# Logsumexp over heads: two of 64 tiles loaded through GpSimd in parts of 120 and 8 rows, each batch stored in one DMA

## Chip, cores, metric

One core of a Trainium2 chip. The metric is the device time of one execution, in microseconds.

## The reference

```python
def reference(x, bias):            # x [8, 2048, 2048] f32, bias [8, 256] f32
    x_heads = x.reshape(B, S, H, Dh).transpose(0, 2, 1, 3) + bias[None, :, None, :]
    x_tiled = np.repeat(x_heads, 2, axis=2)
    mx = x_tiled.max(axis=-1, keepdims=True)
    return mx.squeeze(-1) + np.log(np.exp(x_tiled - mx).sum(axis=-1))   # [8, 8, 4096]
```

Per row and head it is the logarithm of the sum of 256 exponentials, and each result is written twice. 134 MB are read from HBM, the chip's main memory, and 1 MB is written, so the loads of x are most of the traffic.

## The kernel before

x is cut into 64 tiles of 256 rows. A tile is `[128 partitions, 2 rows, 2048]` f32, 2 MB, so each partition receives 16 KB that lie together in HBM. The tile lies in SBUF, the on-chip memory of 128 partitions. There are 9 tile buffers. Loads and stores are issued by SyncE (SP).

```python
NBUF = 9
STORE_ROWS = [                      # one list per batch: rows of each store, 64 in all
    [15, 14, 13, 12, 10],
    [11, 9, 16, 16, 12],
    [16, 16, 16, 8, 8],
    ...
]
def load(t):
    for k0, k1, c0, c1 in pieces(t):            # one piece, but for the last two tiles
        nc.sync.dma_start(out=xts[t % NBUF][:, k0:k1, c0:c1], in_=rows_of(t)[:, k0:k1, c0:c1])
...
for t in range(NBUF):
    load(t)
...
def finish(b, src, n_blk, k_rows, base, i, engine):     # once per batch of 8 tiles
    ...                             # transpose on TensorE, logarithm on ScalarE into rs
        step, parts = n, STORE_ROWS[b]
    for rows in parts:              # one DMA each, rows of 2 KB
        ...
        engine.dma_start(out=ov, in_=iv)
...
for t in range(T):
    # TensorE adds the bias to the first two heads of the tile; ScalarE takes exp of
    # everything and sums those two heads; VectorE weighs and sums the other six heads
    ...
            for k in range(k0, k1):
                for c in range(w0, c1, Dh):
                    weigh(xt[:, k, c : c + Dh], c // Dh, sum_at(k, c // Dh))
    if t + NBUF < T:
        load(t + NBUF)
```

The softmax here doesn't subtract the row's maximum and nothing guards it: scores larger than these inputs give would overflow.

## Time and profile before

| | before |
|---|---|
| median of 2 runs | 342.58 us (342.24 to 342.92) |
| span in the profile | 341.4 us |
| load of one tile, undisturbed | 4.89 us, 428 GB/s |
| ScalarE's work on one tile | 4.44 us |
| last load of tile 61 lands | 321.5 us; then 19.9 us of computation |

From the page of the kernel before: the span; the busy share of the 16 DMA engines (in tenths) and the GB/s they moved, in 40 equal slices; the chain of work that ended last, by line; and ScalarE's exponential (busy us, mean ns of one, idle before it and what ended that). In all views PE is TensorE, ACT ScalarE, DVE VectorE, POOL GpSimd, and SPq the queue of SyncE.

```profile
span 341.4 us, 3425 instructions
...
DMA  8999999999999999999999999999999999999910
GB/s 302 430 430 429 427 430 427 426 425 426 424 429 429 430 429 419 431 426 429 430 424 425 428 428 427 379 402 428 430 419 389 397 428 429 396 380 397 366 57 16
...
DMA xt<-in_x_dram 39%; PE ps L160 2%; ACT xt L174 2%; ACT ps L166 1%; ACT res L209 0%; DVE junk L180 0%; SPq L100 0%; PE ps L155 0%; PE tps L196 0%; DVE Rz L180 0%; ACTq L174 0%; DVEq L318 0%
...
L174 ACT ACTIVATE xt<-xt 128x3072 f32<-128x3072 f32 (+3 forms) x70 | 177.7, 2541 | 24.5 <-DMA xt<-in_x_dram 19.9
```

The engines are busy until the last two slices and move about 428 GB/s, but for some dips late in the run. The exponential waited for little but loads.

One more record matters. The page counts 16 DMA engines, and in the trace each load of 128 rows has 16 completion events. They are read here as one of each engine, so that a lagging engine shows up as one event behind the others (in the table by 1.11 us at tile 8 and by 7.81 us at tile 61):

```
completion of a tile's load, us behind the median of its 16 engines, kernel before
tile   median    the four slowest engines
   8    47.33    0.27  0.39  0.75  1.11
  18    96.27    0.39  0.76  1.74  3.08
  42   214.73    0.93  1.29  2.29  8.18
  61   313.68    1.68  2.17  2.22  7.81
```

### The profile page before, as it was taken

Reading aid. Unit: us, or ns where it says so; the run is one execution under the profiler, and the core shown is the slowest. Engines: PE = TensorE matmul, PEld = TensorE weight load, DVE = VectorE, ACT = ScalarE, POOL = GpSimd, SP = SyncE. Lnnn points to the kernel's source line nnn. Section 1 sums busy time; section 2 is a strip of 40 time slices with the busy share of each in tenths; the row PEclk is TensorE's granted clock in tenths of the full one; section 3 lists DMA queues with packets and bytes.
Section 4 is the critical chain, followed back from the end, with each engine's and each line's share of the span. In section 5 each row is a group of like instructions: output and inputs, shape, how many; then the busy total and the mean of one; then the engine's idle time right before and its main releaser. Section 6 shows DMA issues by size and latency. Waiting matters only on the chain. (4 is left out here: it accounts for less than half of the span.)

```text
span 341.4 us, 3425 instructions
## 1 busy us (share of the span) xinstructions
PE 235.2 (69%) x410; PEld 69.7 (20%) x410; DVE 271.6 (80%) x1538; ACT 295.2 (86%) x597; POOL 10.4 (3%) x22
## 2 busy tenths in 40 slices
PE   6295788767786767775767775965775665775791
PEld 2121122112121112221121221321221221221220
DVE  0429999898887888887889688787798698797795
ACT  2389999998997998987997997998998998998895
POOL 6000000000000000000000000000000000000004
PEclk9999856885868885888885886588888888888585
DMA  8999999999999999999999999999999999999910
GB/s 302 430 430 429 427 430 427 426 425 426 424 429 429 430 429 419 431 426 429 430 424 425 428 428 427 379 402 428 430 419 389 397 428 429 396 380 397 366 57 16
DMA packets 11545, 135.50 MB, mean 397 GB/s; under 512 B 1913, under 2 KB 2185, under 8 KB 3329
## 3 DMA queue, kind: packets, MB, share of 16 engines
q1 hardware_dynamic: 11168, 135.17, 94.8%
q0 software_dynamic: 352, 0.10, 0.1%
q14 instruction: 20, 0.16, 0.1%
q8 instruction: 3, 0.05, 0.1%
q10 hardware_dynamic: 2, 0.01, 0.0%
HBM read 134.23 MB, written 1.05 MB: 396 GB/s over the span
## 5 line engine op out<-in xcount | busy, mean ns | idle before, releaser
L180 DVE CUSTOM_DVE_ANT_0 junk<-xt,w_rep 128x256 f32<-128x256 f32 x768 | 270.8, 422 | 65.7 <-ACT xt L174 65.6
L160 PE MATMUL ps<-xt,ident 128*128 128x512 f32 x256 | 184.3, 859 | 88.6 <-DMA xt<-in_x_dram 88.3
L174 ACT ACTIVATE xt<-xt 128x3072 f32<-128x3072 f32 (+3 forms) x70 | 177.7, 2541 | 24.5 <-DMA xt<-in_x_dram 19.9
L166 ACT ACTIVATE ps<-ps 128x256 f32<-128x256 f32 x256 | 94.6, 369 | 11.7 <-PE ps L160 6.7
L160 PEld LDWEIGHTS ps<-xt,ident 128*128 128x128 f32 x256 | 57.4, 248 | 173.2 <-DMA xt<-in_x_dram 124.2
L180 DVE DVE_READ_ACCUMULATOR2_ANT R<- 128x1 f32 x744 | 61.9, 83 | 0.0
L155 PE MATMUL ps<-b,ones 3*128 3x512 bf16 x128 | 46.6, 447 | 6.2 <-DVE R L180 6.2
L166 ACT ACTIVATION_READ_ACCUMULATOR ps<-ps 128x1 f32 x256 | 48.6, 190 | 0.0
L155 PEld LDWEIGHTS <-ones 3*128 3x128 bf16 x128 | 7.5, 97 | 74.5 <-issue 66.7
L230 POOL DMA_DIRECT2D out_dram<-res x8 | 4.0, 505 | 324.1 <-ACT res L209 324.1
L136 PE MATMUL ps<-brow,ones 1*128 1x512 f32 x6 | 5.5, 1074 | 3.2 <-DMA brow<-in_bias_dram 3.2
L209 ACT ACTIVATE res<-tps 64x512 f32<-64x512 f32 (+3 forms) x11 | 5.9, 540 | 1.4 <-PE tps L196 0.9
L143 ACT ACTIVATE w_rep<-ps 128x512 f32<-128x512 f32 x3 | 1.8, 597 | 5.5 <-PE ps L136 5.5
L196 PEld LDWEIGHTS tps<-ident,R 128*64 128x64 f32 (+1 forms) x16 | 2.7, 166 | 8.9 <-issue 4.7
L196 PE MATMUL tps<-ident,R 128*64 128x128 f32 (+1 forms) x16 | 4.3, 363 | 0.0
L196 PE MATMUL tps<-ident,Rz 128*8 128x128 f32 x2 | 0.7, 374 | 4.7 <-DVE Rz L180 4.7
L136 PEld LDWEIGHTS ps<-brow,ones 1*128 1x128 f32 x6 | 1.8, 321 | 5.3 <-issue 5.3
L110 ACT ACT_TABLE_LOAD x1 | 1.3, 1283 | 0.7 <-PEq L307 0.7
L132 POOL DMA_DIRECT2D b<-bparts x3 | 1.6, 553 | 0.0
L196 PEld LDWEIGHTS tps<-ident,Rz 128*8 128x8 f32 x2 | 0.2, 82 | 5.2 <-DVE Rz L180 2.6
L129 POOL TENSOR_TENSOR brest<-brest,bparts 1x512 f32<-1x512 f32 x1 | 1.1, 1146 | 0.1
L127 POOL TENSOR_TENSOR brest<-brow,bparts 1x512 f32<-1x512 f32 x1 | 1.1, 1144 | 0.1
(15 smaller groups left out, 5.7 us busy)
## 6 DMA issues: line engine op xcount, KB each, us to landing
xt<-in_x_dram SPq DMA_DIRECT2D x62, 2048.0 KB
xt<-in_x_dram SPq DMA_DIRECT2D x2, 1024.0 KB
xt<-in_x_dram SPq DMA_DIRECT2D x2, 512.0 KB
xt<-in_x_dram SPq DMA_DIRECT2D x3, 256.0 KB
out_dram<-res SPq DMA_DIRECT2D x17, 32.0 KB
xt<-in_x_dram SPq DMA_DIRECT2D x2, 128.0 KB
out_dram<-res POOLq DMA_DIRECT2D x8, 12.0 KB, 1.7
out_dram<-res SPq DMA_DIRECT2D x3, 24.0 KB
```

Source lines behind the costliest of these rows:

```text
L110: nc.scalar.add_instruction(mybir.InstLoadActFuncSet(name=nc.get_next_instruction_name(), act_func_set_id=set_idx,))
L132: nc.gpsimd.dma_start(out=b3[i : i + 1, :], in_=bparts[:, i])
L136: nc.tensor.matmul(ps[i], lhsT=ones, rhs=brow[:, CPE + c : CPE + c + MM], start=True, stop=True,)
L143: nc.scalar.activation(out=w_rep[:, c : c + MM], in_=ps[i], func=ACT.Exp)
L155: nc.tensor.matmul(p[:, 0:CPE], lhsT=ones3, rhs=b3, start=True, stop=False)
L160: nc.tensor.matmul(p[:, 0:CPE], lhsT=ident, rhs=v, start=False, stop=True)
L166: nc.scalar.activation(out=p[:, c : c + Dh], in_=p[:, c : c + Dh], func=ACT.Exp, accum_out=dst(h),)
L174: nc.scalar.activation(out=v, in_=v, func=ACT.Exp)
L180: nc.vector.tensor_tensor_reduce(out=j, in0=v, in1=w_rep[:, c : c + Dh], scale=1.0, scalar=0.0, op0=ALU.mult, op1=ALU.add, accum_out=dst,)
L196: nc.tensor.transpose(out=tps[i][0:nr, k], in_=src(k), identity=ident)
L209: nc.scalar.activation(out=rv, in_=tv, func=ACT.Ln)
L230: engine.dma_start(out=ov, in_=iv)
```

## The change

The intent can be read from the code. Its constant `SLOW = 3` names one DMA engine as the slow one. GpSimd is to load two tiles so that this engine gets no part of them: 120 rows to the other 15 engines, and the last 8 rows, too, to others. The code counts in `turn`, modulo 16, where it supposes GpSimd's next row to go, and short "filler" DMAs are to turn that count to the right place. Four fillers on SP are added, and each batch is stored in one DMA of 64 rows.

```diff
+SPECIAL = (16, 40)
+SLOW = 3
...
+    fill = [sb.tile([16, 160], F32, name=f"fill{i}") for i in range(8)]
...
+    def turn_by(engine, rows):
+        i = turn[1]
+        turn[1] += 1
+        n = 128 + i
+        engine.dma_start(out=fill[i][0:rows, 0:n], in_=x[0, 0:rows, 0:n])
+
+    def turn_to(at):
+        if (at - turn[0]) % 16:
+            turn_by(nc.gpsimd, (at - turn[0]) % 16)
+        turn[0] = at
+
+    def load_special(t):
+        dst, src = xts[t % NBUF], rows_of(t)
+        cut = P - P // 16
+        turn_to(SLOW + 1)
+        nc.gpsimd.dma_start(out=dst[0:cut], in_=src[0:cut])
+        turn[0] = SLOW
+        turn_to(SLOW + 1)
+        nc.gpsimd.dma_start(out=dst[cut:P], in_=src[cut:P])
+        turn[0] = SLOW + 1 + P - cut
+        if t == SPECIAL[0]:
+            for rows in (1, 2, 3, 4):
+                turn_by(nc.sync, rows)
+
     def load(t):
+        if t in SPECIAL:
+            load_special(t)
+            return
...
-            step, parts = n, STORE_ROWS[b]
+            step, parts = n, [nr]
```

More of the change, by code (lines that the diff above doesn't have):

```diff
@@ L22 @@
 LAST_CUTS = [[0, 1024, 2048], [0, 512, 1024, 1536, 1792, 2048]]
-STORE_ROWS = [
-    [15, 14, 13, 12, 10],
-    [11, 9, 16, 16, 12],
-    [16, 16, 16, 8, 8],
-    [16, 16, 16, 9, 7],
-    [16, 16, 16, 10, 6],
-    [16, 16, 16, 11, 5],
-    [16, 16, 16, 12, 4],
-]
+SPECIAL = (16, 40)
+SLOW = 3
 @with_exitstack
@@ L96, in rows_of @@
         return v.rearrange("(k p) d -> p k d", k=K)
+    turn = [0, 0]
+    def turn_by(engine, rows):
[19 more added lines that the diff above has]
+                turn_by(nc.sync, rows)
     def load(t):
+        if t in SPECIAL:
+            load_special(t)
+            return
         for k0, k1, c0, c1 in pieces(t):
```

## The prediction

> **What bounds the kernel now.** The DMA engines, and among them one straggler. The slice view shows them nine tenths busy until the last stores; the chain of waits is mostly "DMA xt<-in_x_dram". In the instruction records ScalarE needs 4.44 us per tile unheld, but its period is 4.89 us, idling on the load before most tiles from 14 on: compute has slack, the loads have not.
>
> The completion events of the loads (16 per load, one per engine) show the straggler. A tile takes 4.89 us on every engine, yet one engine lands last in every tile: 1.1 us after the median at 33 us, 3.1 at 77 us, 5.2 at 141 us, 8.2 at 214 us. The lag grows in steps of about 1.0 us each 25 us. The instruction-fetch packets (queue 14, 8 KB) recur at the same beat (54, 76, 101, 127, 154 us), which fits VectorE's 1538 instructions. [...]Tile 61 lands at 321.5 us, at 313.7 in the median and 315.9 on the next slowest engine. From 321.5 on ScalarE waits on no load for the last 20 us. So the straggler sets the time.
>
> Which engine is it? It completes also in the stores of 5 and 4 rows[...].
>
> **What the change does.** [...]Each skip spares the straggler 8 packets of 611 ns, 4.9 us. Single stores take its rows per batch from 5 to 4, about 0.7 us in all, and free issue slots: only 8 SP loads and stores may be in flight, and bursts of 5 stores now cost the fast engines 0.3 to 1.2 us of stall at each batch from 215 us on. That is off the critical path while the straggler leads.
>
> **A doubt.** In the built program the one-row fillers of 129 and 135 elements are split as 3x43 and 15x9[...]. No trace here decides.
>
> **Sum**, for the landing of tile 61, with a tail of 20 us unchanged:
> - one skip: 321.5 - 4.9 - 0.7 = 315.9; time about 337 us (likeliest)
> - two skips: straggler 311, but the second slowest engine, freed of stalls, 313.5 to 314; about 335
> - none: about 342.5
>
> Tiles 16 and 40 arrive early and delay their neighbours by up to 4.9 us; ScalarE wins that back at 0.45 us per tile.
>
> **Predicted: 337.0 us, 334.3 to 343.3.** Chances: faster by over 2% 0.22, within 2% 0.74, slower 0.04.
>
> **What would show it.** Right: the straggler's lag drops by 4.9 us at tile 16 (perhaps at 40), tile 61 lands near 316, the tail stays 20 us, fast engines' stalls at batch ends vanish. Wrong: the lag grows through both tiles as before (another engine skipped), or GpSimd's tile packets take more than 611 ns, or ScalarE is still behind after tile 55.

The sum comes to 321.5 - 4.9 - 0.7 = 315.9 us for the landing of tile 61, hence, with the tail of 20 us and the 1.2 us by which the time of the kernel before exceeds its span, to about 337 us. Its numbers stand, as estimates: 4.9 us are 8 packets of 611 ns, the 128 packets of a tile over 16 engines; 0.7 us is about one store row less for the straggler in each of 8 batches, at the 84 ns that a packet of 2 KB took in the median in the kernel before. The 4 rows per batch are 64 rows over the 16 completions that such a store has in the kernel after; the 5 were seen in the kernel before, as the straggler completes in every store of a batch. It is the last even in the store of 5 rows (8.16 us behind the median) and in that of 4 (1.00 us).

## More of the kernel before

The windows of the kernel before around the place of the first changed tile (last two columns: busy share of the DMA engines, GB/s):

```profile
...
core 0: us, PE busy (x) PEld busy (x) DVE busy (x) ACT busy (x) POOL busy (x), PEclk, DMA share, GB/s
40.00:58.00 18.00, 14.74 (x24) 4.07 (x22) 17.19 (x99) 17.75 (x37) 0.00 (x0) 0.62 1.01 428
58.00:80.00 22.00, 13.46 (x27) 3.73 (x26) 20.50 (x117) 20.63 (x47) 0.00 (x0) 0.81 1.01 428
80.00:98.00 18.00, 14.95 (x25) 4.51 (x26) 14.66 (x83) 16.93 (x31) 0.00 (x0) 0.69 1.00 426
```

And from its timeline of ScalarE, the exponentials of four tiles in that stretch (a bracket, where there is one, gives the idle time before):

```profile
...
start us, us, engine line op out<-in xcount [idle before <-releaser]
...
65.38 2.75 ACT L174 ACTIVATE xt<-xt 128x3072 f32<-128x3072 f32 x1
...
69.82 2.75 ACT L174 ACTIVATE xt<-xt 128x3072 f32<-128x3072 f32 x1
...
74.26 2.75 ACT L174 ACTIVATE xt<-xt 128x3072 f32<-128x3072 f32 x1
...
79.85 2.77 ACT L174 ACTIVATE xt<-xt 128x3072 f32<-128x3072 f32 x1 [1.05 <-DMA xt<-in_x_dram]
```

## The result

362.11 us, median of 2 runs (362.01 to 362.21), against 342.58 us: the ratio is 1.057, with a 95% interval of 1.0523 to 1.0617. The change made the kernel 5.7% slower.

The same lines of the page, of the kernel after:

```profile
span 360.2 us, 3415 instructions
...
DMA  8999999999999999999999999999999999999510
GB/s 307 425 433 430 430 421 338 227 246 425 423 430 426 427 430 428 428 426 425 429 429 247 245 337 431 425 430 428 428 430 428 428 424 428 427 427 403 234 52 16
...
DMA xt<-in_x_dram 76%; ACT xt L198 11%; ACT ps L190 5%; PE ps L160 2%; PE ps L184 1%; DVE junk L204 1%; DMA out_dram<-res 1%; DMA brow<-in_bias_dram 1%; ACT res L233 0%; PE ps L179 0%; ACT w_rep L167 0%; PE tps L220 0%; ACTq L198 0%; SPq L1
...
L198 ACT ACTIVATE xt<-xt 128x3072 f32<-128x3072 f32 (+3 forms) x70 | 177.5, 2539 | 44.6 <-DMA xt<-in_x_dram 43.8
```

The GB/s row has two holes that were not there before: slices 7 to 9 and 22 to 24 (from 54 and from 189 us) fall to 227 to 338 GB/s. Between the first slice and the tail it is elsewhere at 420 to 433 GB/s, and the late dips of the kernel before have gone. The busy row shows nothing of it: in the holes, too, the engines are busy at nine tenths. The windows say it more sharply:

```profile
...
core 0: us, PE busy (x) PEld busy (x) DVE busy (x) ACT busy (x) POOL busy (x), PEclk, DMA share, GB/s
40.00:58.00 18.00, 14.64 (x23) 4.00 (x22) 17.20 (x99) 17.75 (x37) 2.00 (x4) 0.62 1.01 431
58.00:80.00 22.00, 7.33 (x11) 2.28 (x10) 9.17 (x53) 10.33 (x22) 0.00 (x0) 0.65 1.02 241
80.00:98.00 18.00, 12.11 (x18) 3.41 (x18) 12.44 (x72) 13.17 (x26) 0.00 (x0) 0.59 0.99 416
```

From 58 to 80 us the DMA engines were busy all the time (a share of 1.02 against 1.01 before), and moved 241 GB/s instead of 428. So packets (the single transfers of which a load consists) became longer; the DMA engines did not wait for work. The timeline of ScalarE shows what this did to the computation:

```profile
...
start us, us, engine line op out<-in xcount [idle before <-releaser]
...
60.86 2.76 ACT L198 ACTIVATE xt<-xt 128x3072 f32<-128x3072 f32 x1
...
65.22 0.20 ACT L190 ACTIVATION_READ_ACCUMULATOR ps<-ps 128x1 f32 x1
76.93 2.76 ACT L198 ACTIVATE xt<-xt 128x3072 f32<-128x3072 f32 x1 [11.51 <-DMA xt<-in_x_dram]
...
84.64 2.76 ACT L198 ACTIVATE xt<-xt 128x3072 f32<-128x3072 f32 x1 [2.95 <-DMA xt<-in_x_dram]
...
90.56 2.76 ACT L198 ACTIVATE xt<-xt 128x3072 f32<-128x3072 f32 x1 [1.16 <-DMA xt<-in_x_dram]
```

ScalarE stood still for 11.51 us, then for 2.95 us, waiting for a load. In the second hole it waited 8.49 and 7.10 us.

The queues and the loads of the kernel after, from its page (bytes and share of the engines' time by queue; then each kind of load with its size and time to landing):

```profile
...
q1 hardware_dynamic: 10564, 130.98, 89.3%
q0 software_dynamic: 832, 4.30, 5.2%
...
xt<-in_x_dram SPq DMA_DIRECT2D x60, 2048.0 KB, 35.4
xt<-in_x_dram POOLq DMA_DIRECT2D x2, 1920.0 KB, 21.9
...
xt<-in_x_dram POOLq DMA_DIRECT2D x2, 128.0 KB, 25.9
```

The second queue carried 4.30 MB of 135, that is 3.2% of the bytes, but its packets took 5.2% of the engines' time. In the records of single packets:

```
packets of 16 KB between 20 and 310 us, ns: 5%, median, 95%
kernel after, GpSimd's queue    871  1115  1429
kernel after, SP's queue        611   613   744
```

Inside the first hole, from 60 to 78 us, the packets of SP's ordinary loads are slow too: 1.05 us in the median.

The tail is as it was: the load of tile 61 lands at 340.5 us (before: 321.5), and 19.7 us of computation follow (before: 19.9). All of the loss comes before that point.

### The profile page after: what moved, and what is told of

It is laid out like the page before. It is cut to its first block, busy times and chain, and to the rows that moved or that the text cites. A ratio compares the mean times of both kernels' runs of the same rounds, so it can differ in the third digit from the quotient of the medians.

```text
span 360.2 us, 3415 instructions
## 1 busy us (share of the span) xinstructions
PE 235.7 (65%) x410; PEld 69.1 (19%) x410; DVE 271.6 (75%) x1538; ACT 293.8 (82%) x597; POOL 14.3 (4%) x30
## 3 DMA queue, kind: packets, MB, share of 16 engines
HBM read 134.24 MB, written 1.05 MB: 376 GB/s over the span
## 4 chain that ended last, share of the span: by engine, by line
DMA 77%; ACT 17%; PE 3%; DVE 1%; issue 1%; another core or an unknown queue 0%; ACTq 0%; SPq 0%; DVEq 0%
DMA xt<-in_x_dram 76%; ACT xt L198 11%; ACT ps L190 5%; PE ps L160 2%; PE ps L184 1%; DVE junk L204 1%; DMA out_dram<-res 1%; DMA brow<-in_bias_dram 1%; ACT res L233 0%; PE ps L179 0%; ACT w_rep L167 0%; PE tps L220 0%; ACTq L198 0%; SPq L124 0%
## 5 line engine op out<-in xcount | busy, mean ns | idle before, releaser
L179 PE MATMUL ps<-b,ones 3*128 3x512 bf16 x128 | 48.2, 461 | 6.5 <-DVE R L204 6.5
L110 POOL DMA_DIRECT2D xt<-in_x_dram x2 | 1.1, 525 | 173.8 <-PE ps L179 128.3
L99 POOL DMA_DIRECT2D fill<-in_x_dram x4 | 2.0, 502 | 0.0
```

The lines of the kernel that those rows point to most:

```text
L99: engine.dma_start(out=fill[i][0:rows, 0:n], in_=x[0, 0:rows, 0:n])
L179: nc.tensor.matmul(p[:, 0:CPE], lhsT=ones3, rhs=b3, start=True, stop=False)
```

## The experiments

Two things might cost the time in the holes. The theory of the split: a tile that is loaded in DMAs of fewer than 128 rows, such as 120 and 8, is slow to load, whichever queue they come from. (In the recorded texts it had the name of a mechanism that no trace shows; name and mechanism are cut there.) The theory of mixing: packets of two queues alternate on each engine, or GpSimd's descriptors are slow. A third candidate is the other half of the change, the stores. All comparisons below are with the kernel before on the same chip in the same rounds. Experiments 1 to 4 ran on one chip, 5, 6, 8 and 9 on a second, 7 and 10 on a third, so experiments are compared with each other by their ratios.

| run | median us | ratio to before | 95% interval |
|---|---|---|---|
| after (the change) | 362.11 | 1.057 | 1.0523 to 1.0617 |
| single stores alone | 341.57 | 0.9951 | 0.9938 to 0.9964 |
| GpSimd loads alone | 364.47 | 1.062 | 1.0587 to 1.0653 |
| GpSimd, 128 rows in one DMA | 341.36 | 0.9948 | 0.9929 to 0.9967 |
| 120 and 8 rows from SP | 366.98 | 1.069 | 1.0671 to 1.0709 |
| two halves from SP | 364.37 | 1.0634 | 1.0594 to 1.0674 |
| change without fillers | 363.79 | 1.0609 | 1.0589 to 1.063 |
| half the VectorE instructions (wrong result) | 335.94 | 0.9803 | 0.9787 to 0.9818 |
| single stores, four batches 51 + 13 | 340.56 | 0.9931 | 0.9919 to 0.9944 |
| four tiles in a row in halves | 366.00 | 1.0666 | 1.0647 to 1.0684 |
| single stores, six batches 51 + 13 | 340.23 | 0.992 | 0.9906 to 0.9933 |

The results of all but the marked one were correct.

### 1. Single stores alone

```diff
 # the kernel before
-            step, parts = n, STORE_ROWS[b]
+            step, parts = n, [nr]
```

> The kernel before with one store per batch and nothing else of the change. Theory (the slowdown lies wholly in the two GpSimd loads): the straggling DMA engine has 4 instead of 5 store rows per batch, so 341.5 to 342.5 us, the same as before or 0.2% faster, and the median engine no longer stalls at batch ends. Rival (the single 128 KB store of 64 rows costs time of its own, by holding up the loads behind it): slower by some 2 to 3 us per batch, up to 362 us.

Measured: 341.57 us, ratio 0.9951. The stores are the good half of the change. The row of GB/s of this run has no dips left before the end:

```profile
...
GB/s 306 427 428 429 427 430 423 430 428 425 432 423 427 426 432 423 432 426 427 432 426 426 424 430 429 429 425 424 430 428 430 425 428 427 431 426 411 196 50 17
```

In the kernel before, at most 8 DMAs of SP are in flight: in the trace each is issued only after the one eight places earlier has landed (the store issued at 69.04 us after the load that landed at 69.02 us). So a burst of five stores leaves few loads queued, and engines that are ahead run dry: after the burst of stores issued from 228 to 249 us two loads of a tile complete 5.4 and 5.5 us after the one before them on the median engine, instead of 4.89 us. With one store per batch the dips are gone. It seems to take the lag as well as the burst: experiment 8 keeps the five stores, its straggler lags by at most some 6 us, and its row of GB/s stays above 415 up to 300 us. But that is not what shortens the run: the straggler's load of tile 61 lands at 320.2 instead of 321.5 us, while the median engine gains far more, 308.6 against 313.7 us. The gain of 1.3 us there is more than the 0.7 us estimated for a store row less per batch; why was not tested.

### 2. The GpSimd loads alone

```diff
 # the change
-            step, parts = n, [nr]
+            step, parts = n, STORE_ROWS[b]
```

> The change without its single stores: the two loads through GpSimd with all filler rows, and the stores of before. Theory: all of the slowdown is here, 361 to 364 us, and the two stretches of some 22 us with half the bandwidth are there again.[...] Rival (single stores slow it): 342 us or less.

Measured: 364.47 us, ratio 1.062: the whole of the loss is here. This run also tells which engine was spared, from the completions that are present in each DMA (an SP DMA of fewer than 16 rows has one more event, early, at its issue: in the kernel after the filler of 3 rows has 4 events and that of 4 rows 5; it is left out of the row, though not of the median):

```
completions of successive SP DMAs, us behind the median, this run
tile 15, 128 rows     -4.61 -0.77 ...  0.82  3.09     (16 engines)
filler, 3 rows        -0.06  0.06  0.09               no straggler
filler, 4 rows        -0.12  0.00  0.03  2.01         the straggler is the fourth
tile 18, 128 rows     -4.63 -0.77 ...  0.83  3.11     (16 engines)
store, 15 rows        -0.80 -0.68 ...  0.80  3.09     the one ahead is missing
```

SP DMAs of 2, 3 and 4 rows give 2, 3 and 4 completions, and the straggler is present with 4 rows and absent with 3. The engine that runs ahead after the special load, the spared one, is another: on tile 18 it is 4.63 us ahead while the straggler is 3.11 us behind, and in the store of 15 rows it is missing while the straggler is there. The trace does not number the engines; whether the straggler is number 3, as the code has it, was not shown. In the kernel after one engine is 4.3 us ahead of the median after the first special load and 9.4 us after the second, so it is the same one twice. In the first load of 120 rows itself one completion comes 8.22 us before the median and the other 15 within 0.44 us of it.

### 3. Whole tiles through GpSimd

```diff
     def load_special(t):
-        ...                     # all of it: fillers, 120 rows, fillers, 8 rows
+        nc.gpsimd.dma_start(out=xts[t % NBUF], in_=rows_of(t))
```

> The change with the two tiles loaded through GpSimd as one DMA of 128 rows each, no filler rows on either queue. [...]no collapse, packets near 611 ns during the two loads, 341 to 344 us. Rival of mixing (packets of GpSimd's and SP's queues alternating on an engine cost some 0.45 us per change of queue, whatever the rows): two stretches of half bandwidth, some 10 us each, 361 us or more.

(The 0.45 us are the author's estimate; the 1.05 us of a packet in the hole less the 0.61 us of others come near it.)

Measured: 341.36 us, ratio 0.9948, the same as single stores alone (0.9951). In the packet records GpSimd's 256 packets took 611 to 619 ns (5% to 95%). The windows of this run, in which the packets of GpSimd's first tile run from 59 to 69 us:

```profile
...
core 0: us, PE busy (x) PEld busy (x) DVE busy (x) ACT busy (x) POOL busy (x), PEclk, DMA share, GB/s
40.00:58.00 18.00, 14.15 (x25) 3.89 (x23) 17.20 (x99) 17.75 (x37) 0.56 (x1) 0.69 1.01 428
58.00:80.00 22.00, 15.46 (x21) 4.72 (x21) 17.49 (x99) 18.57 (x38) 0.00 (x0) 0.58 1.01 427
80.00:98.00 18.00, 14.41 (x29) 4.02 (x27) 14.85 (x85) 16.18 (x35) 0.00 (x0) 0.82 1.00 426
```

427 GB/s in the same window. From 58 to 68 us 127 packets of GpSimd's queue and 132 of SP's start side by side, as they did in the kernel after, and 4.30 MB pass through GpSimd's queue as they did there, now in 3.1% of the engines' time instead of 5.2%:

```profile
...
q0 software_dynamic: 640, 4.30, 3.1%
```

Mixing and GpSimd's descriptors are out.

### 4. The same parts, issued from SP

```diff
     def load_special(t):
-        turn_to(SLOW + 1)
-        nc.gpsimd.dma_start(out=dst[0:cut], in_=src[0:cut])
-        ...
-        nc.gpsimd.dma_start(out=dst[cut:P], in_=src[cut:P])
-        ...                     # and no filler on SP
+        nc.sync.dma_start(out=dst[0:cut], in_=src[0:cut])
+        nc.sync.dma_start(out=dst[cut:P], in_=src[cut:P])
```

> The change with the parts of 120 and 8 rows issued from SP, no GpSimd load and no filler rows. [...]packets go to about 1.2 us during these loads, each load costs some 5 us, 350 to 354 us. Rival of mixing, or of GpSimd's descriptors: one queue alone, so packets stay at 611 ns and the time at 341 to 343 us.

(The 1.2 us and the 5 us are estimates from half the bandwidth, seen in the holes of the change as 241 GB/s against 428: twice the 611 ns of a packet, and once more the 4.89 us of a tile.)

Measured: 366.98 us, ratio 1.069. The holes are there with no GpSimd load at all; they come later, as the load stands in line behind the others in SP's queue:

```profile
...
core 0: us, PE busy (x) PEld busy (x) DVE busy (x) ACT busy (x) POOL busy (x), PEclk, DMA share, GB/s
40.00:58.00 18.00, 14.81 (x25) 4.06 (x23) 17.19 (x99) 17.75 (x37) 0.00 (x0) 0.68 1.00 426
58.00:80.00 22.00, 16.44 (x25) 5.06 (x26) 20.52 (x117) 21.48 (x47) 0.00 (x0) 0.66 1.01 426
80.00:98.00 18.00, 9.09 (x12) 2.20 (x11) 10.39 (x60) 8.80 (x18) 0.00 (x0) 0.50 1.02 238
```

```profile
...
GB/s 305 425 431 429 431 431 430 428 404 216 269 431 425 429 429 424 431 425 430 428 429 422 390 211 310 399 427 431 422 428 431 428 428 422 428 405 276 68 49 15
```

The kind of result is that of the split; the size is not: 12.7 us per tile (1.069 less 0.9951, of 343.16 us, halved), where 5 were expected. Experiment 7 takes that up.

### 5. Halves of 64 rows: equal parts

```diff
     def load_special(t):
-        ...
+        for r in (0, P // 2):
+            nc.sync.dma_start(out=dst[r : r + P // 2], in_=src[r : r + P // 2])
```

> The change with each of the two tiles loaded from SP as two halves of 64 rows, no GpSimd load, no filler rows. [...]packets of about 1.2 us during these loads, at least 4.9 us lost per tile, 350 to 365 us. Rival (it is the uneven share, 15 or 8 engines instead of 16, that costs): same as with single stores alone, 341 to 342 us.

Measured: 364.37 us, ratio 1.0634, 11.7 us per tile. Here the two parts of a tile are equal. The holes of this run:

```profile
...
GB/s 306 425 434 431 429 424 427 428 415 202 293 432 422 427 429 427 427 429 427 433 425 424 403 199 303 400 429 427 430 426 428 432 428 419 434 417 316 75 49 15
```

So it is not the unequal size of the parts: two equal halves cost 11.7 us per tile, 120 and 8 rows 12.7. (That each engine has the same share of the halves was the author's reading and was not shown.) Nor is it the mere number of DMAs: every run loads tile 62 in two DMAs of 1 MB, but of 128 partitions each, and in the kernel before the median engine completes them 2.5 us apart, 420 GB/s. What the loads of 64 and 120 rows have in common, and those of 128 rows have not, is that one DMA writes only some of the partitions. In the middle of the holes the slices of the change and of experiments 4 and 5 show 199 to 247 GB/s, and in the first hole of the two experiments the median packet of 16 KB took 1.27 us instead of 0.61. Why was not shown: the trace does not tell which partitions an engine writes, and another split may also change which addresses of HBM are read at the same time; no run changed one without the other.

### 6. The change without fillers

```diff
     def load_special(t):
-        turn_to(SLOW + 1)
         nc.gpsimd.dma_start(out=dst[0:cut], in_=src[0:cut])
-        turn[0] = SLOW
-        turn_to(SLOW + 1)
         nc.gpsimd.dma_start(out=dst[cut:P], in_=src[cut:P])
-        ...                     # and no filler on SP
```

> The change without any filler row on either queue; the 120 and 8 rows still go through GpSimd. Theory ([...]fillers move nothing): 360 to 363 us, and one engine ahead by 4 to 5 us after each such load, as in the change. Rival (the fillers cost, by their issue slots and their place in the queue): some us faster than the change, 355 us or less.

Measured: 363.79 us; one engine is ahead by 4.3 us after the first special load and by 9.4 us after the second, as with fillers. It is 1.7 us over the change, in other rounds and with overlapping intervals. Fillers neither steer these loads nor cost anything that shows.

### 7. Four tiles in a row, each in halves

```diff
 # experiment 5
-SPECIAL = (16, 40)
+SPECIAL = (16, 17, 18, 19)
```

> As the run with halves on SP, but tiles 16 to 19, four in a row, are each loaded in two halves of 64 rows. It asks why a tile loaded so costs 11.4 us[...]. Theory of transition (the neighbours of a halved tile are slowed as well, since engines come out of step at its start and end; within a run of halved tiles each costs 4.9 us): 11.4 + 3 x 4.9 = 26 us over single stores alone, about 368 us. Theory of the single tile (each halved tile costs its 11.4 us wherever it stands): 4 x 11.4 = 46 us, about 387 us.

Measured: 366.00 us, ratio 1.0666, that is 24.5 us over single stores alone (1.0666 less 0.9951, of 343.27 us), near the 26 us of the theory of transition. One hole, longer:

```profile
...
GB/s 310 429 432 427 426 428 429 428 406 196 221 216 230 276 424 427 420 433 431 426 425 430 425 428 427 422 435 433 423 425 431 430 428 426 424 429 408 151 52 15
```

The completion events tell more than the mean of 11.7 us for a lone tile (11.4 us in the recorded text, as half the difference of the profiled spans, 362.6 and 339.9 us, gives). This is how much later than in the run with single stores alone the loads complete (up to tile 12 the three runs agree within 0.2 us):

```
us later than with single stores alone         straggler   median engine
experiment 5, after tile 16                       9.5          7.8
experiment 5, after tile 40                      22.0         15.9
experiment 7, after tiles 16 to 19               23.9         21.9
```

At the same place, tile 16, one halved tile costs 9.5 us and four in a row 23.9: each further one adds 4.8 us. So a halved tile costs about its own 4.9 us once more, plus some 4.6 us where such tiles begin and end. There its packets would meet those of normal tiles on other engines, since the engines are some us apart (the straggler was 2.6 us behind the median before tile 16). That the neighbours are slowed there is argued from this difference; which packets lose how much is left open. The tile at 40 cost 12.5 us, 3 us more than that at 16, and it was the straggler that lost these 3 us (the median engine lost 7.8 and 8.1 us). It lagged by 8.5 us before tile 40 and by 2.6 us before tile 16, which may be why; that was not tested.

### 8. Half of VectorE's instructions (wrong result)

Was the premise right, that the straggler alone sets the time, and lags because it fetches VectorE's instructions?

```diff
 # the kernel before; two heads in one instruction of 512 columns
-                for c in range(w0, c1, Dh):
-                    weigh(xt[:, k, c : c + Dh], c // Dh, sum_at(k, c // Dh))
+                w = 2 * Dh if left > 1 else Dh
+                for c in range(w0, c1, w):
+                    weigh(xt[:, k, c : c + w], c // Dh, sum_at(k, c // Dh))
```

(`weigh` takes its width from the view; the sums that are no longer written are set to 1 at the start.)

> Wrong result on purpose. The kernel before, but VectorE weighs two heads in one instruction of 512 columns, so it has about half the instructions for the same elements; loads and stores are those of before. Theory (the straggling engine is the one that fetches VectorE's instructions, and it alone sets the time): the straggler's steps of 1.0 us come about every 50 us instead of 25, its lag ends near half, and the time falls by 4 to 6 us to 336.5 to 339 us. Rival (the straggler lags for another reason): steps and time unchanged, 342 to 343.5 us.

Measured: 335.94 us, ratio 0.9803. With 794 instead of 1538 VectorE instructions the straggler's completion of tile 61 comes at 315.0 us (before: 321.5), 6.1 us behind the median, and the tail is 19.2 us. The steps are seen in the packet records: in the kernel before a fetch of 8 KB at the beat takes 0.31 to 0.33 us, and once in each beat one 16 KB packet takes 1273 ns (once 1259) instead of 611, which together makes the step of 1.0 us.

```
16 KB packets of over 1.2 us, start in us, up to 212 us
kernel before         32.0  54.4  76.8  101.4  127.5  153.9  182.8  208.3
half the instructions 41.7  85.5  133.4  179.2
```

The premise holds: with half the VectorE instructions, and half the slow packets (4 instead of 8), the straggler's load of tile 61 lands 6.5 us sooner and the run is 6.8 us shorter. That the fetches are on the straggler is inferred from the common beat (fetches at 54.1, 76.5, 101.1 us, slow packets at 54.4, 76.8, 101.4 us); the packet records name no engine. The change just does not relieve it.

### 9 and 10. Stores that spare the straggler

In experiment 2 the straggler was absent from a DMA of 3 rows on SP. 51 is 3 times 17, and the author guessed that a store of 51 rows has the same three engines. By that guess the straggler has 1 row instead of 4 in such a batch, which at 84 ns for a packet of 2 KB is an estimate of 0.25 us, or 1.0 us over four batches.

```diff
 # single stores alone
-            step, parts = n, [nr]
+            step, parts = n, ([51, 13] if b % 2 == 0 else [nr])          # experiment 9
+            step, parts = n, ([51, 13] if b not in (3, 6) else [nr])     # experiment 10
```

> Single stores, but every second batch in two stores of 51 and 13 rows. [...]Theory[...]: 0.5 to 1.2 us faster than with single stores alone, that is 340.3 to 341.3 us against a kernel before of 343. Rival[...]: the same or slower than single stores alone.

Measured: 340.56 us, ratio 0.9931. The store of 51 rows has three completions of engines, none of them the straggler's. At the end of this run the slowest of the three was 6.7 us behind the median and the straggler 10.2 us, so six such batches seemed to have room.

> As the run with stores of 51 and 13 rows, but in six batches of eight instead of four. Theory[...]: 0.3 to 0.6 us faster, about 340.1 us. Rival[...]: the same or slower than with four batches.

Measured: 340.23 us, ratio 0.992. The interval (0.9906 to 0.9933) lies clear of that of single stores alone (0.9938 to 0.9964); the interval with four batches overlaps both, so it is told apart from neither. This is the fastest correct version, 0.8% under the kernel before, and a much smaller step than the 2% of experiment 8.

## Why the prediction was wrong

- **The bound: right.** The straggler sets the time; relieving it moves the end (experiment 8), and 19 to 20 us of computation follow the landing of tile 61 in all four runs in which it was read (before, after, experiments 1 and 8).
- **The stores: right in kind.** They free the fast engines and win little. Expected 0.7 us, measured 1.3 us at tile 61 and a ratio of 0.9951.
- **The step that failed: that the special loads skip the straggler, and "Each skip spares the straggler 8 packets of 611 ns, 4.9 us".** The first half rested on a supposition about the engines that GpSimd chooses, which no trace had shown. It failed in the way that the sum has as "none": another engine was spared, the same one both times, and without fillers one was ahead by the same 4.3 and 9.4 us (experiments 2 and 6). The straggler was not relieved: its lag at tile 61 was 11.4 us, against 11.6 us with single stores alone. By the prediction's own sum that alone would have meant about 342.5 us. The second half failed more heavily, as it priced the packets of a 120-row load at the 611 ns of a 128-row load. They took 1115 ns in the median, and in the first hole the packets of the ordinary loads beside them took 1.05 us. In the sum, a term of -4.9 us was in truth about +10 us per tile: 320.2 us for tile 61 with single stores alone, 340.5 us with the change, over two tiles.
- **What was foreseen and underrated.** "GpSimd's tile packets take more than 611 ns" stood among the signs of being wrong, but slower by over 2% was given a chance of 0.04. In the profile of the kernel before, every load of x has 128 rows, so it could not show it.
- **The arithmetic of a neighbour.** Even with half the bandwidth known, one would have estimated 4.9 us more per tile, its own 4.89 us once more (10 us in all), not 20. Lone tiles of that kind cost 9.5 us and more, by what happens at their edges, as experiment 7 argues.

## What to carry to other kernels

Load 128 partitions in one DMA, or measure what a split costs: here a load of 120 and 8 rows, from GpSimd or from SP, or of 2 x 64 rows from SP moved the same bytes at about half the bandwidth (199 to 247 GB/s in the middle of the holes, against 428). A full DMA busy row does not mean full bandwidth (a busy share of 1.02 at 241 GB/s), so read the row of GB/s beside it and ask for the length of single packets. Before steering work away from one engine, show by completion events which engine was in fact spared.
